# Two weight panels over one token chunk at the head of a decoder step

## The chip, the cores and the metric

The kernel runs on one core of a Trainium2 chip. The metric is the device time of one execution in microseconds (us). A core has a matrix engine (TensorE, PE in the profile, with its weight loads as PEld), a vector engine (DVE), a scalar engine (ACT), GpSimd (POOL) and SyncE (SP), whose queue issues the DMA transfers of this part of the kernel. Each engine works through its own queue in order and waits there for the work of others.

## The reference

One inference step of a decoder layer over 1024 prompt tokens and 8 x 8 sample tokens, with D_MODEL = 1024:

```python
u = rmsnorm(x);  [a | q | k | v | g_a | g_b] = u @ w_in
# branch A: causal pooling of a (4 groups of 128 channels, windows 2/4/8/16),
#           (mean - a) -> linear map per group -> scale -> @ w_pa
# branch B: dilated window attention on q, k, v -> @ w_pb
h = x + (sigmoid(g_a) * A + sigmoid(g_b) * B) @ w_o
y = h + relu(rmsnorm(h) @ w_up)^2 @ w_down
```

The part that matters here is `a`, the pooling input: 512 channels, that is two panels of 256 columns of w_in, for all 1088 tokens. The row norm of x is not applied before the product: x is scaled by the norm weight alone, and the factor for each token, taken from its sum of squares, comes in later.

## The kernel before

Features lie on the partitions: x arrives as eight rows of 128 features, each with all tokens, and the tokens are cut into three chunks of 384, 384 and 320 (`CHUNKS`). Every product is made from two-part numbers: ACT makes a rounded "high" copy and DVE the rest, "low", of each operand, and PE does three passes (high x high, high x low, low x high: `PASSES`). For x this is `split_x` (lines 297 and 298, one row of one chunk each), for weights `split` (lines 114 and 115, one raw tile of 512 columns, that is two feature rows of a panel).

A panel of w_in comes in four raw tiles (line 123), which rotate through three buffers, and its halves are kept in one of three `places`. For the first panel `panel` calls `first(j)` between the fetch and the split of each raw tile: it loads the two x rows that belong to it and splits them. Row 0 and the small table `cols` are loaded ahead (lines 278 and 279), row 1 by line 304, the others in pairs by line 281.

`pool_input(ja, wt, c)` multiplies one panel by one chunk: for each pair of feature rows 12 matmuls (line 319: three passes, two column halves m, two rows kk), 48 for the whole. They collect in two PSUM banks of the four `acc` banks, and `pool_evac` copies these to `ext` on ACT (lines 331 and 336).

The order on PE is the order of the code. It is: twelve warm-up matmuls on `ones` (line 345); panel 0 on chunks 0, 1, 2; panel 1 on chunks 0, 1, 2; then the first products of the q, k, v panels (lines 611, 614 and 194). Between the chunks of panel 1 stand the token sums `x_sums(c)` (line 354): after chunk 0 `x_sums(0)`, after chunk 1 `x_sums(1)` and a small transpose `wk`, and inside chunk 2, after 36 of its 48 matmuls, `x_sums(2)`.

`x_sums(c)` needs the squares of chunk c. ACT squares x in place (line 289, four instructions for a chunk, held back until the matmuls that stand before them in the code have ended), POOL adds the four up (line 291, three for a chunk). PE then sums over the partitions into three small PSUM tiles `rt`, which all three calls share; DVE reads them (line 358, `xms`), and POOL makes the power of it (line 359, `rtok`). `sample_rows` copies the sample tokens on DVE (line 269).

The queues of ACT, DVE, POOL and SP are not written by hand: a scheduler lays them out when the kernel is built, from a model of the timeline, and the order is then fixed.

Of the kernel before, what the change touches and what calls it, by code (L numbers as in the profile page):

```python
# [7 lines left out]
F32 = mybir.dt.float32  # L8
# [7 lines left out]
P = 128  # L16
# [4 lines left out]
KD = D // P  # L21
CH = 384
CHUNKS = ((0, 384), (384, 384), (768, 320))
# [13 lines left out]
def decoder_step(ctx, tc, i, o):  # L37
    nc = tc.nc
    v_, s_, g_, t_ = nc.vector, nc.scalar, nc.gpsimd, nc.tensor
    dma = nc.sync.dma_start  # L40
    dma_st = nc.sync.dma_start

    def pool(name, bufs=1, **kw):
        return ctx.enter_context(tc.tile_pool(name=name, bufs=bufs, **kw))
# [44 lines left out]
    def part4(c):  # L89

        return slice(CHUNKS[c][0] // 4, (CHUNKS[c][0] + CHUNKS[c][1]) // 4)
# [16 lines left out]
    wp = pool("w")  # L108
    places = wp.tile([P, 3, 2, 2048], F32R, name="places")
    place = [0]  # L110
    throttle = []

    def split(dst_hi, dst_lo, src):
        ins = s_.activation(dst_hi, src, AF.Copy)
        v_.tensor_tensor(dst_lo, src, dst_hi.bitcast(F32), op=ALU.subtract)  # L115
        return ins
# [43 lines left out]
    def panel(src, name, between=None, after=None):  # L160

        n = src.shape[1]
        wt = places[:, place[0] % 3]
        place[0] += 1
        for a in range(0, n, 512):
            raw = fetch(src, name, a)
            if between is not None:
                between(a // 512)
            ins = split(wt[:, 0, a:a + 512], wt[:, 1, a:a + 512], raw)
            if after is not None:  # L170
                behind_pe(ins, after[a // 512])
        throttle.append(ins)
        return wt

    def by_k(wt, kb=KD):
        return wt.rearrange("p s (k n) -> p s k n", k=kb)
# [59 lines left out]
    def acc_tile(name, tag="acc", bufs=4):  # L236
        return rr(acc_p, [P, 512], F32, name, tag, bufs)
# [55 lines left out]
    def split_x(c, k):  # L293
        c0, n = CHUNKS[c]
        hi, lo = (act4[s][k][:, :, part4(c)] for s in range(2))
        x = xs[c, k].rearrange("p (l r) -> p r l", r=4)
        s_.activation(hi, x, AF.Copy, scale=ln1[:, k:k + 1])  # L297
        v_.scalar_tensor_tensor(lo, x, ln1[:, k:k + 1], hi.bitcast(F32), op0=ALU.mult, op1=ALU.subtract)

    def first(j):  # L300
        if j:
            load_x(0, j)
        else:
            dma(xs[0, 1], i["xT"][:, 1, :CH])
        split_x(0, 2 * j)
        split_x(0, 2 * j + 1)

    L = 15 + SEQ
    LS = L + NB * 23
# [2 lines left out]
    def pool_input(ja, wt, c, middle=None):  # L312
        c0, n = CHUNKS[c]
        pts = [acc_tile(f"a{2 * ja + m}_{c}") for m in range(2)]
        for k in range(0, KD, 2):
            for p, (a, b) in enumerate(PASSES):
                for m in range(2):
                    for kk in (k, k + 1):
                        last_mm[0] = t_.matmul(  # L319
                            pts[m][:, :n], wt[:, a, kk, m * P:(m + 1) * P], act4[b][kk][:, :, part4(c)],  # L320
                            start=(p == 0 and kk == 0), stop=(p == 2 and kk == KD - 1))
            if middle and k == 4:
                middle()
        return pts

    def pool_evac(ja, c, pts):
        c0, n = CHUNKS[c]
        for m in range(2):
            ext = exts[2 * ja + m]
            npr = min(n, SEQ - c0)  # L330
            s_.copy(ext[:, 15 + c0:15 + c0 + npr].rearrange("p (l r) -> p l r", r=4),
                    from4(pts[m][:, :n])[:, :npr // 4])
            if npr < n:
                new = from4(pts[m][:, :n])[:, npr // 4:].rearrange("p (t q) r -> p q r t", q=2)
                for q in range(2):
                    s_.copy(ext[:, L:].rearrange("p (b t) -> p b t", b=NB)[:, 4 * q:4 * q + 4, 15:], new[:, q])

    def open_ext(g):
        exts[g] = rr(xp, [P, LS], F32, name=f"ext{g}", tag="ext", bufs=4)
        v_.memset(exts[g][:, :15], 0.0)  # L340


    wu = rr(ps, [P, 512], F32, name="wu", tag="wu", bufs=1)[:, :P]
    for _ in range(12):
        t_.matmul(wu, ones, ones, start=True, stop=True)
    load_x(0, 0)
    wt = by_k(panel(i["w_in"][0], "a0", first))
    def x_sums(c):
        n = CHUNKS[c][1]
        rt = [rr(ps, [P, 1], F32, name=f"rt{c}_{b}", tag="rt", bufs=3) for b in range(3)]  # L350
        for b in range(3):
            w = min(P, n - b * P)
            for k in range(2):
                t_.matmul(rt[b][:w], xs[c, 6 + k][:, b * P:b * P + w], ones[:, :1], start=(k == 0), stop=(k == 1))
        for b in range(3):
            w = min(P, n - b * P)
            col = slice(3 * c + b, 3 * c + b + 1)
            v_.tensor_scalar(xms[:w, col], rt[b][:w], 1.0 / D, EPS, op0=ALU.mult, op1=ALU.add)
            g_.tensor_tensor(rtok[0][:w, col], xms[:w, col], mhalf[:w, :1], op=ALU.pow)
            v_.tensor_scalar(xeps[0][:w, col], xms[:w, col], EPS, None, op0=ALU.mult)  # L360
# [36 lines left out]
    for c in range(3):  # L397
        if c < 2:
            for j in range(4):
                load_x(c + 1, j)  # L400
        if c == 0:
            open_ext(0)
            open_ext(1)
        pool_evac(0, c, pool_input(0, wt, c))
        if c < 2:
            for k in range(KD):
                split_x(c + 1, k)
        if c:
            square_x(c - 1)
    square_x(2)  # L410
    w1 = by_k(panel(i["w_in"][1], "a1"))
    dma(cst, i["consts"])
    v_.tensor_scalar(wqs, wqc, HD ** -0.5, None, op0=ALU.mult)
    dma(states, i["stateT"].rearrange("g p b t -> p g (b t)"))
    kn = win("kn")[:, :P]
    for g in range(3):
        dma(kn[2 * g:2 * g + 2], i["qk_norm"][g, 1].rearrange("(j d) -> j d", j=2))
    open_ext(2)
    open_ext(3)
    for c in range(3):  # L420
        pool_evac(1, c, pool_input(1, w1, c, (lambda: x_sums(2)) if c == 2 else None))
        if c == 0:
            x_sums(0)
            sample_rows()
        if c == 1:
            x_sums(1)

            wk = rr(ps, [P, 512], F32, name="wk", tag="wu", bufs=1)[:, :6]
            t_.transpose(wk, kn[:6], ident[:6, :6])
            v_.tensor_tensor(wqk, wqs, wk, op=ALU.mult)  # L430
# [676 lines left out]
    for g in (2, 1, 0):  # L1107
# [39 lines left out]
        for blks in ((8, 0), (1,), (2,), (3,), (4,), (5,)) + (((6, 7),) if g else ((6,), (7,))):  # L1147
# [10 lines left out]
            for js in (((0, 1), (2,)) if blks[0] in (1, 2, 3, 4, 5) else ((0,), (1,), (2,))):  # L1158
                for b in (blks[::-1] if g == 0 and js == (2,) else blks):
# [307 lines left out]
    for n, (f, a) in enumerate(order):  # L1467
# [5 lines left out]
        t = row_tile(1 + a, f)  # L1473
# [187 lines left out]
    for j in range(2):  # L1661
        for d in range(4):
            wt = by_k(panel(i["w_o"][d], f"o{j}{d}"))
# [251 lines left out]
    kept, hs, rows, chain = {}, {}, {}, []  # L1915
# [246 lines left out]
```

## Time and profile before

| what | us |
|---|---|
| time, median of 3 runs | 1431.8 (1431.59 to 1432.39) |
| the profiled execution, its own time | 1434.28 |
| its span, first to last instruction | 1432.1 |
| PE busy in the span | 1410.9 |
| DVE busy | 976.4 |
| ACT busy | 758.7 |
| POOL busy | 225.5 |

Times in the profile count from the start of the span. The profiled execution is 2.5 us above the median of the runs and its span is 2.2 us shorter than its own time. PE is busy for 99% of the span, but busy time of pipelined matmuls says nothing on whether they follow one another closely; for the head of the kernel the instructions themselves have to be read.

### The profile page before, as it was taken

The page shows a single profiled execution, that of the slowest core. Times are in us where ns is not written, and L with a number is a line of the kernel's source. Part 1 is how long each engine was busy: PE and PEld are TensorE (multiplying, and loading weights), DVE is VectorE, ACT ScalarE, POOL GpSimd, SP SyncE. Part 2 cuts the span into 40 slices and gives each one's busy share as a digit, 9 for nine tenths or more (in the row PEclk, how much of TensorE's full clock was granted, in tenths as well). Part 3 has the DMA queues.
Part 4 walks back from the last instruction along what each step waited for, and adds up shares of the span by engine and source line. Part 5 has one row for each costly group of instructions (what it writes and reads, how often), then busy time and mean ns, then how long its engine had stood idle before and what let it go on. Part 6 is the DMA issues. An engine that isn't in the chain of part 4 may idle for free.

```text
span 1432.1 us, 29419 instructions
## 1 busy us (share of the span) xinstructions
PE 1410.9 (99%) x11101; PEld 1358.0 (95%) x11101; DVE 976.4 (68%) x1795; ACT 758.7 (53%) x1962; POOL 225.5 (16%) x291
## 2 busy tenths in 40 slices
PE   9999999999989999999999999999999999999998
PEld 8988977887989999999999999999999999999998
DVE  7688675676768677786468876666665686664556
ACT  8557755687755233573336545554554544444442
POOL 0711255565400000000001000000000000000100
PEclk9999999999999999999999999999999999999999
DMA  6322888854576686974558667656658987777684
GB/s 211 115 80 108 222 210 213 199 134 113 127 226 213 207 260 192 331 265 151 168 174 256 231 221 230 210 203 230 224 189 283 319 272 257 234 241 222 208 279 155
DMA packets 184204, 300.01 MB, mean 209 GB/s; under 512 B 34423, under 2 KB 91069, under 8 KB 182014
## 3 DMA queue, kind: packets, MB, share of 16 engines
q1 hardware_dynamic: 180990, 254.49, 57.5%
q0 software_dynamic: 3072, 43.65, 9.3%
q8 instruction: 87, 1.43, 0.4%
q14 instruction: 55, 0.45, 0.1%
HBM read 229.66 MB, written 112.06 MB: 239 GB/s over the span
## 4 chain that ended last, share of the span: by engine, by line
PE 85%; DMA 6%; DVE 4%; ACT 2%; issue 2%; SPq 1%; POOL 1%; DVEq 0%; ACTq 0%; POOLq 0%
PE pz L1249 22%; PE pd L2021 21%; PE pg L1249 10%; PE ph L194 7%; PE pqk L194 6%; PE pv L194 4%; PE a L319 3%; PE pab L1567 2%; PE pq L194 1%; PE pk L194 1%; DMA gg<-g_d 1%; DMA gv<-ts_d 1%; DVE places L115 1%; DVE act L115 1%; DMA out_yT_dram<-row 1%
## 5 line engine op out<-in xcount | busy, mean ns | idle before, releaser
L2021 PE MATMUL pd<-places 128*128 128x272 f32 x2688 | 335.2, 287 | 1.4 <-DVE places L1257 1.0
L2021 PEld LDWEIGHTS pd<-places 128*128 128x128 f32 x2688 | 334.7, 188 | 1.8 <-DVE places L1257 1.2
L1256 ACT ACTIVATE places<-raw_d 128x544 fp32r<-128x544 f32 (+1 forms) x176 | 111.0, 646 | 156.4 <-DMA raw_d<-z_d 48.3
L1257 DVE TENSOR_TENSOR places<-raw_d,places 128x544 fp32r<-128x544 f32 (+1 forms) x176 | 122.5, 710 | 88.5 <-ACT places L1256 87.3
L2060 POOL DMA_DIRECT2D out_kv_sample_dram<-in_cache_kv_dram x96 | 47.0, 490 | 832.0 <-ACT places L1256 538.0
L1249 PE MATMUL pz<-act,places 128*128 128x272 f32 x912 | 119.2, 289 | 0.0
L1249 PEld LDWEIGHTS pz<-act,places 128*128 128x128 f32 x912 | 116.5, 188 | 0.0
L194 PE MATMUL ph<-act,places 128*128 128x272 f32 x768 | 97.0, 288 | 0.0
L194 PEld LDWEIGHTS ph<-act,places 128*128 128x128 f32 x768 | 96.5, 188 | 0.1
L1249 PE MATMUL pg<-act,places 128*128 128x272 f32 x576 | 79.8, 297 | 2.4 <-ACT g L1475 2.4
L1249 PE MATMUL pz<-act,apart 128*128 128x272 f32 x624 | 82.0, 289 | 0.0
L1249 PEld LDWEIGHTS pz<-act,apart 128*128 128x128 f32 x624 | 79.9, 188 | 0.1
L1249 PEld LDWEIGHTS pg<-act,places 128*128 128x128 f32 x576 | 76.4, 195 | 3.2 <-ACT g L1475 2.6
L634 POOL TENSOR_TENSOR mr<-ms,mhalf 128x4 f32<-128x4 f32 (+2 forms) x39 | 54.1, 1387 | 109.7 <-DVE ms L633 109.6
L194 PE MATMUL pqk<-places,act 128*128 128x512 f32 x240 | 61.0, 403 | 0.0
L1249 PE MATMUL pz<-places 128*128 128x272 f32 x432 | 56.4, 287 | 0.0
L1249 PEld LDWEIGHTS pz<-places 128*128 128x128 f32 x432 | 55.0, 188 | 0.0
L839 POOL TENSOR_TENSOR pck<-pck,qs 128x256 f32<-128x256 f32 x64 | 48.4, 788 | 36.7 <-DMA pck<-in_cache_kv_dram 22.0
L194 PEld LDWEIGHTS pqk<-places,act 128*128 128x128 f32 x240 | 44.6, 192 | 9.9 <-issue 0.2
L319 PE MATMUL a<-act,places 128*128 128x384 f32 (+1 forms) x288 | 50.5, 332 | 1.1 <-ACT act L297 1.1
L1567 PE MATMUL pab<-ab,places 128*128 128x272 f32 x384 | 50.5, 287 | 0.0
L319 PEld LDWEIGHTS a<-act,places 128*128 128x128 f32 x288 | 47.5, 188 | 3.0 <-ACT act L297 1.9
(438 smaller groups left out, 2864.2 us busy)
## 6 DMA issues: line engine op xcount, KB each, us to landing
out_kv_sample_dram<-in_cache_kv_dram POOLq DMA_DIRECT2D x72, 480.0 KB, 4.9
raw_d<-z_d SPq DMA_DIRECT2D x112, 272.0 KB
z_d<-t SPq DMA_DIRECT2D x84, 272.0 KB
raw_d<-in_w_down_dram SPq DMA_DIRECT2D x80, 256.0 KB
raw_u<-in_w_up_dram SPq DMA_DIRECT2D x64, 256.0 KB
raw_qkv<-in_w_in_dram SPq DMA_DIRECT2D x36, 256.0 KB
pck<-in_cache_kv_dram SPq DMA_DIRECT2D x32, 256.0 KB
pcv<-in_cache_kv_dram SPq DMA_DIRECT2D x32, 256.0 KB
```

The costliest lines, as they stand in the source:

```text
L115: v_.tensor_tensor(dst_lo, src, dst_hi.bitcast(F32), op=ALU.subtract)
L194: last_mm[0] = t_.matmul(out, lhs(a, k), rhs(b, k), start=(j == 0), stop=(j == len(terms) - 1))
L319: last_mm[0] = t_.matmul(pts[m][:, :n], wt[:, a, kk, m * P:(m + 1) * P], act4[b][kk][:, :, part4(c)], start=(p == 0 and kk == 0), stop=(p ...
L634: g_.tensor_tensor(r[:n, :H], ms[:n, :H], mhalf[:n, :H], op=ALU.pow)
L839: behind_pe(g_.tensor_tensor(t[:, n], t[:, n], qs[:, :256], op=ALU.mult))
L1249: last_mm[0] = t_.matmul(x[c][:, :Q], A[:, a, k * P:(k + 1) * P], Bv(b, k, c), start=(first and n == 0), stop=(n == len(terms) - 1), skip_ ...
L1256: ins = s_.activation(view(t[:, 0]), src, AF.Copy)
L1257: v_.tensor_tensor(view(t[:, 1]), src, view(t[:, 0]).bitcast(F32), op=ALU.subtract)
L1567: last_mm[0] = t_.matmul(q[x][:, c, :Q], w.rearrange("p s n -> p (s n)")[:, at:at + P], rhs, start=(n == 0), stop=(n == len(terms) - 1))
L2021: last_mm[0] = t_.matmul(chain[t][:, c, :Q], A[:, a, t * P:(t + 1) * P], Z[:, b, c * Q:(c + 1) * Q], start=(fresh and f == 0 and n == 0), ...
L2060: ins = g_.dma_start(d, a)
```

## The change

The two panels of `a` are loaded in turns, raw tile by raw tile, and both multiply chunk 0 together: for each pair of feature rows the 12 matmuls of panel 0, then the 12 of panel 1. Chunk 0 so takes four PSUM banks. Then panel 0 does chunks 1 and 2, and panel 1 chunks 1 and 2. The very first raw tile is loaded and split in two halves of one feature row each; x row 0 is split with the first half, and x row 1 is loaded behind both halves and split with the second. For that first pair of panel 0 the 12 matmuls go row by row: six for row 0, six for row 1. There are ten warm-up matmuls. `x_sums(0)` moves to the middle of panel 1 on chunk 1, `x_sums(1)` and `sample_rows` follow after that chunk, and `x_sums(2)` stays in the middle of chunk 2.

```diff
-    def first(j):
+    def first(j, rows):
         if j:
             load_x(0, j)
-        else:
+        elif 1 in rows:
             dma(xs[0, 1], i["xT"][:, 1, :CH])
-        split_x(0, 2 * j)
-        split_x(0, 2 * j + 1)
+        for m in rows:
+            split_x(0, 2 * j + m)
...
         for k in range(0, KD, 2):
+            pool_terms(pts, wt, c, k)
+            if middle and k == 4:
+                middle()
+        return pts
+
+    def pool_terms(pts, wt, c, k, by_row=False):
+        n = CHUNKS[c][1]
+        for ks in ((k,), (k + 1,)) if by_row else ((k, k + 1),):
             for p, (a, b) in enumerate(PASSES):
                 for m in range(2):
-                    for kk in (k, k + 1):
+                    for kk in ks:
...
-    for _ in range(12):
+    for _ in range(10):
         t_.matmul(wu, ones, ones, start=True, stop=True)
     load_x(0, 0)
-    wt = by_k(panel(i["w_in"][0], "a0", first))
+    two_wide = [places[:, n] for n in range(2)]
+    place[0] = 2
+    for n in range(4):
+        for j in range(2):
+            raw = rr(wp, [P, 512], F32, name=f"raw_a{j}_{n}", tag="raw", bufs=3)
+            parts = (slice(0, 256), slice(256, 512)) if n + j == 0 else (slice(0, 512),)
+            for cs in parts:
+                dma(raw[:, cs], i["w_in"][j][:, 512 * n + cs.start:512 * n + cs.stop])
+            for m, cs in enumerate(parts):
+                if j == 0:
+                    first(n, (m,) if parts[1:] else (0, 1))
+                split(*(two_wide[j][:, s, 512 * n + cs.start:512 * n + cs.stop] for s in range(2)), raw[:, cs])
+    wt, w1 = (by_k(t) for t in two_wide)
...
         if c == 0:
-            open_ext(0)
-            open_ext(1)
-        pool_evac(0, c, pool_input(0, wt, c))
+            for g in range(4):
+                open_ext(g)
+            pts = [acc_tile(f"a{m}_0") for m in range(4)]
+            for k in range(0, KD, 2):
+                for j, w in enumerate((wt, w1)):
+                    pool_terms(pts[2 * j:2 * j + 2], w, 0, k, k + j == 0)
+            for j in range(2):
+                pool_evac(j, 0, pts[2 * j:2 * j + 2])
+        else:
+            pool_evac(0, c, pool_input(0, wt, c))
...
-    w1 = by_k(panel(i["w_in"][1], "a1"))
...
-    for c in range(3):
-        pool_evac(1, c, pool_input(1, w1, c, (lambda: x_sums(2)) if c == 2 else None))
-        if c == 0:
-            x_sums(0)
+    for c in (1, 2):
+        pool_evac(1, c, pool_input(1, w1, c, lambda: x_sums(2 if c == 2 else 0)))
+        if c == 1:
             sample_rows()
-        if c == 1:
             x_sums(1)
```

More of the change, by code (lines that the diff above doesn't have):

```diff
@@ L321, in pool_input @@
                             start=(p == 0 and kk == 0), stop=(p == 2 and kk == KD - 1))
-            if middle and k == 4:
-                middle()
-        return pts
     def pool_evac(ja, c, pts):
@@ L417, in decoder_step @@
         dma(kn[2 * g:2 * g + 2], i["qk_norm"][g, 1].rearrange("(j d) -> j d", j=2))
-    open_ext(2)
-    open_ext(3)
-    for c in range(3):
-        pool_evac(1, c, pool_input(1, w1, c, (lambda: x_sums(2)) if c == 2 else None))
-        if c == 0:
-            x_sums(0)
+    for c in (1, 2):
+        pool_evac(1, c, pool_input(1, w1, c, lambda: x_sums(2 if c == 2 else 0)))
+        if c == 1:
             sample_rows()
-        if c == 1:
             x_sums(1)
```

## The prediction

> **What bounds the kernel now.** I read the page first: the chain that ended last is PE's for 85% of the span. Then I read that chain in order of time over the first 85 us, where the change lies (columns: start, us, what).
>
> ```profile
> PE 85%; DMA 6%; DVE 4%; ACT 2%; issue 2%; SPq 1%; POOL 1%; DVEq 0%; ACTq 0%; POOLq 0%
> ...
> 3.09 5.59 DMA xs<-in_xT_dram
> 8.70 1.86 ACT act L297 x2
> 10.60 30.83 PE a L319 x179
> 41.43 1.23 PE rt L354 x12
> 42.66 8.64 PE a L319 x48
> ...
> 59.27 1.96 PE a L319 x12
> ```
>
> Up to 10.6 us the chain is x rows 2 and 3: their transfer, then their two high copies. From there it does not leave PE until the pooling input ends at 61.2 us. So the head ends when PE's matmuls end, and time can be won only where PE waits among them. The weight loads, in order of time, show where; they break wherever a matmul had to wait (start, length, engine, line, instruction, count, idle before).
>
> ```profile
> 1.06 5.13 PEld L345 LDWEIGHTS wu<-ones 128*128 128x128 f32 x24 [1.06 <-DVE ones L73]
> 6.15 0.19 PEld L319 LDWEIGHTS a<-act,places 128*128 128x128 f32 x1
> 7.24 0.65 PEld L319 LDWEIGHTS a<-act,places 128*128 128x128 f32 x4 [0.90 <-ACT act L297]
> 8.19 1.18 PEld L319 LDWEIGHTS a<-act,places 128*128 128x128 f32 x7 [0.30 <-DVE act L298]
> 9.73 0.19 PEld L319 LDWEIGHTS a<-act,places 128*128 128x128 f32 x1 [0.37 <-ACT act L297]
> 10.60 0.65 PEld L319 LDWEIGHTS a<-act,places 128*128 128x128 f32 x4 [0.68 <-ACT act L297]
> 11.55 2.04 PEld L319 LDWEIGHTS a<-act,places 128*128 128x128 f32 x12 [0.30 <-DVE act L298]
> 13.86 1.17 PEld L319 LDWEIGHTS a<-act,places 128*128 128x128 f32 x7 [0.27 <-DVE act L298]
> 15.18 25.93 PEld L319 LDWEIGHTS a<-act,places 128*128 128x128 f32 x156 [0.15 <-ACT places L114]
> ...
> 52.62 5.28 PEld L319 LDWEIGHTS a<-act,places 128*128 128x128 f32 x36
> 57.86 1.33 PEld L354 LDWEIGHTS rt<-ones,xs 128*128 128x128 f32 x12
> ```
>
> From 15.18 us on PE is dense. The 36 loads in 5.28 us are of the 320-token chunk: 0.147 us each. Of the 156 loads in 25.93 us, 48 are of that chunk (7.06 us), so the other 108, of 384 tokens, take 0.175 each. Ahead of 15.18 lie 1+4+7+1+4+12+7 = 36 matmuls, 6.3 us of dense work. PE therefore behaves **as if it had begun at 15.18 - 6.3 = 8.9 us** and never waited. I call this the dense start. The first matmul starts at 6.15; the 2.7 us between are waits for splits. All of the gain of the head is a lower dense start.
>
> **The change part by part.** No matmul of the product goes away: chunk 0 takes 96 in a row instead of 48 and 48. What changes is when each is ready. ACT, DVE and SP at the start (all from the timeline of the head):
>
> ```profile
> 2.14 0.43 SPq L304 DMA_DIRECT2D xs<-in_xT_dram  x1
> 2.61 0.43 SPq L123 DMA_DIRECT2D raw_a<-in_w_in_dram  x1
> 3.46 0.98 ACT L297 ACTIVATE act<-xs,cols 128x384 fp32r<-128x384 f32 x1 [1.22 <-DMA cols<-in_cols_dram]
> 4.48 0.90 DVE L298 SCALAR_TENSOR_TENSOR act<-xs,cols,act 128x384 fp32r<-128x384 f32 x1 [0.91 <-ACT act L297]
> 5.47 0.63 ACT L114 ACTIVATE places<-raw_a 128x512 fp32r<-128x512 f32 x1 [1.03 <-DMA raw_a<-in_w_in_dram]
> 6.21 0.98 ACT L297 ACTIVATE act<-xs,cols 128x384 fp32r<-128x384 f32 x1
> 8.70 1.85 ACT L297 ACTIVATE act<-xs,cols 128x384 fp32r<-128x384 f32 x2 [0.35 <-DMA xs<-in_xT_dram]
> ```
>
> *Warm-up and first half.* Twenty loads of 0.214 us (5.13 / 24) end at 1.06 + 4.28 = 5.3 us instead of 6.2. Row 0 is split by 4.44 (high) and 5.38 (low). The first half of the weights lands between 3.4 us (the table `cols`, issued before it, was there by 3.46) and 5.47 (the whole tile was). Its high copy costs between half of 0.63 and 0.63; I take 0.37. So six matmuls can go from about 5.4 us. These two edits by themselves give nothing more, since the later rows decide; uncovered, the two warm-ups would be worth 0.9 us.
>
> *Row 1.* Its transfer is issued one slot, 0.47 us, later (behind the second half, at 2.61). Its high copy ran at 6.21, right behind another copy, so it had landed by then; now I take 6.4 (5.9 to 6.7), high done at 7.4, low at 8.3. The ninth matmul is the first that needs the low part, so the dense start is at least 8.3 - 8 x 0.175 = 6.9.
>
> *Rows 2 and 3.* Ahead of their transfer now stands one more weight tile. It costs between one SP slot (0.47 us) and that plus its 256 KB at the rate of the head:
>
> ```profile
> 5.00:10.00 5.00, 4.31 (x21) 3.35 (x19) 2.96 (x5) 3.55 (x5) 0.00 (x0) 1.00 1.01 343
> 10.00:15.00 5.00, 4.58 (x23) 3.82 (x23) 5.00 (x7) 5.00 (x7) 0.00 (x0) 1.00 1.07 377
> ```
>
> At 360 GB/s (last column) that is 0.7 us, so the high copies start between 9.2 and 9.9 instead of 8.70; I take 9.4. Row 3 is then high at 9.4 + 1.85 = 11.25 and low 0.9 later, 12.15. 24 matmuls stand ahead of this pair, so the thirtieth is the first that needs the low part of row 3: dense start 12.15 - 29 x 0.175 = **7.1** (6.9 to 7.6). For later pairs ACT needs 2 x 0.93 + 2 x 0.57 = 3.0 us (1.85 / 2 above, 1.13 / 2 below) and PE has 24 x 0.175 = 4.2 us of work, the 896 KB of a pair and its two weight tiles arrive in 2.5 us, so PE does not wait again in chunk 0. Before, ACT needed 2.4 us for each 2.1 us of PE. That is the mechanism of the gain: **8.9 - 7.1 = 1.8 us**.
>
> *Four banks.* Panel 0 of chunk 1 needs the banks of panel 0 of chunk 0, which end 12 matmuls, 2.1 us, before the chunk does. Their two copies take 0.82 (below). I cost it at nothing; behind other copies on ACT it would be up to 0.8.
>
> *Squares and token sums.* All splits of panel 1 and two more bank copies now stand on ACT ahead of the squares, and POOL's additions hang on these.
>
> ```profile
> 20.35 0.82 ACT L331 COPY ext<-a 128x384 f32<-128x384 f32 x2
> 21.08 7.98 ACT L297 ACTIVATE act<-xs,cols 128x384 fp32r<-128x384 f32 x10
> 30.74 3.04 ACT L289 ACTIVATE xs<-xs 128x768 f32<-128x768 f32 x4
> 33.69 1.13 ACT L114 ACTIVATE places<-raw_a 128x512 fp32r<-128x512 f32 x2
> ...
> 32.40 16.71 POOL L291 TENSOR_TENSOR xs<-xs,xs 128x768 f32<-128x768 f32 x8 [31.95 <-ACT xs L289]
> 49.83 2.55 POOL L359 TENSOR_TENSOR rtok<-xms,mhalf 128x1 f32<-128x1 f32 x3 [0.71 <-DVE xms L358]
> 52.34 2.32 POOL L291 TENSOR_TENSOR xs<-xs,xs 128x640 f32<-128x640 f32 x1
> ```
>
> The squares of chunk 0 started at 30.74. Ahead of them come 1.13 (two splits that were behind), 0.82 (copies) and about 0.1 for the split cut in two, 2.05 us; ACT's waits for x add between 0 and 1.2 us (later transfers, less the split that fills the gap), I take 0.3. They start at 33.1, above PE's gate at 7.1 + 144 x 0.175 = 32.3. POOL's last addition then ends at 52.34 + 2.32 + 2.35 = 57.0, if POOL keeps its order. PE wants it at 57.86 - 1.8 = 56.1. Slack before: 3.2 us; after: none, and a wait of **0.9 us** (0.6 to 1.8).
>
> Sum: -1.8 + 0.9 = **-0.9 us**. Behind the head PE stays the bound, so it passes on to the end. The profiled execution would take 1433.4 us instead of 1434.28; it lies 2.5 above the median of the runs, so I forecast 1430.9. Queues of the later stages may be laid out anew; the largest single wait of PE there is
>
> ```profile
> PE pv L194 <- ACT qk L639: 2.8, 1, 2.8
> ```
>
> so I allow, as an estimate, 1 us to either side.
>
> **The clock.** The warm-up loads take 0.214 us for 128 columns; a later product of the same kind, 2 records of 384 columns in 0.65 us, takes 0.108. PE thus runs at half rate at the start, though the clock column prints 1.00. Later the granted clock (third column from the right) falls to 0.51 for 3.5 us, behind 7 us in which PE was busy for 4.48 only:
>
> ```profile
> 66.65 0.65 PE bcx L244 x2
> ...
> 395.00:402.00 7.00, 4.48 (x47) 4.16 (x45) 2.35 (x8) 1.72 (x6) 0.00 (x0) 1.00 1.06 371
> 402.00:405.50 3.50, 3.50 (x18) 2.95 (x14) 2.90 (x16) 2.36 (x9) 0.00 (x0) 0.51 0.95 241
> ```
>
> [...]
>
> **The rivals.**
>
> *POOL steps aside.* If its powers of chunk 0 (2.55 us) are queued behind the additions, the last one ends by 54.5, before 56.1, and all 1.8 us stay: 1430.0. For it: they become ready later, since `x_sums(0)` moves from 41.4 to 7.1 + 180 x 0.175 + 7.1 = 45.7. Against: one addition stood behind them before.
>
> *A clean start.* If rows 1 to 3 come early enough that PE never waits after the warm-up, the dense start is 5.4 and, with POOL clear, 3.5 us are gained: 1428.3. Against: row 3 must be high 1.5 us sooner than I reckon, with more bytes ahead of it.
>
> *The token sums block PE (slower).* `x_sums(1)` writes the tiles that DVE must have read for chunk 0. Before, 48 matmuls lay between; now 12, 2.1 us.
>
> ```profile
> 34.34 4.63 DVE L115 TENSOR_TENSOR places<-raw_a,places 128x512 fp32r<-128x512 f32 x2 [2.49 <-ACT places L114]
> 49.60 0.15 DVE L358 TENSOR_SCALAR xms<-rt 128x1 f32<-128x1 f32 x1
> ```
>
> DVE read the first at 49.60, 6.9 us after the sums ended at 42.66, being behind splits that took 2.3 us each while POOL added. With the same lag PE waits 6.9 - 2.1 = 4.8 us: -1.8 + 4.8 = +3.0, **1434.8**. It decides from a lag of 3.9 us. Against: fewer splits lie between POOL's start and these sums, which now come 4 us later.
>
> *The clock opens late.* If the shorter warm-up costs one more stretch like that of 402 us, 3.5 us at 0.51, PE loses 1.7 us: +0.8, 1432.6. Against: the waits of 0.90 and 0.68 us did not slow the matmuls then.
>
> **How the numbers follow.** Forecast 0.45, POOL aside 0.20, clean start 0.12, token sums 0.13, clock 0.10. About 0.2%, 2.9 us, is what a measurement of this kernel can tell from no change. Faster by more: most of the clean start, and the edge of POOL aside with the 1 us: 0.20. Slower by more: the token sums and an edge: 0.14. Within: 0.66. The range runs from the clean start less half a microsecond, 1427.8, to just below the token sums' full price, 1434.6; some 0.17 is left out.
>
> **What would show it.** The break in the weight loads for row 3 at about 11.3 to 12.2 us and a long dense run after it give the dense start (7.1); the first squares of ACT at 33 and POOL's last addition at 57 show the give-back, together with an idle time of PE before the third group of `rt` loads. An idle time before the second group would be the token sums blocking. Loads of 0.3 us beyond 6.5 us would be the clock. I am wrong if rows 1 to 3 land elsewhere, or if the scheduler puts POOL's or SP's queue in another order.

## The result: 15 us slower

| | before | after |
|---|---|---|
| median of six runs, us | 1431.86 (1429.9 to 1433.12) | 1447.13 (1443.06 to 1449.19) |
| ratio, 95% interval | | 1.0104 (1.0087 to 1.012) |
| the profiled execution, its own time | 1434.28 | 1445.87 |
| its span | 1432.1 | 1443.7 |

I forecast 1430.9 us, in a range from 1427.8 to 1434.6. The change costs 15.3 us, and both its sign and its size lie outside. First the weight loads of the changed kernel, in order of time (columns as before; L327 is the product of the pooling input, L371 the token sums):

```profile
8.59 3.63 PEld L327 LDWEIGHTS a<-act,places 128*128 128x128 f32 x21 [0.65 <-DVE act L298]
12.52 1.17 PEld L327 LDWEIGHTS a<-act,places 128*128 128x128 f32 x7 [0.30 <-DVE act L298]
13.88 2.03 PEld L327 LDWEIGHTS a<-act,places 128*128 128x128 f32 x12 [0.19 <-ACT places L114]
19.65 6.72 PEld L327 LDWEIGHTS a<-act,places 128*128 128x128 f32 x24 [3.74 <-ACT places L114]
30.37 28.45 PEld L327 LDWEIGHTS a<-act,places 128*128 128x128 f32 x156 [4.00 <-ACT places L114]
...
62.62 1.41 PEld L371 LDWEIGHTS rt<-ones,xs 128*128 128x128 f32 x12 [0.32 <-POOL xs L291]
...
70.26 1.29 PEld L371 LDWEIGHTS rt<-ones,xs 128*128 128x128 f32 x12 [0.78 <-POOL xs L291]
```

Up to 13.88 us the head is what I reckoned with: 36 matmuls lie ahead of that row, so the dense start is 13.88 - 36 x 0.175 = 7.6 us, against 8.9 before. Then two waits of 3.74 and 4.00 us follow, both for the high copies of weights. And the loads behind them are slow: the 24 take 6.72 us instead of 24 x 0.175 = 4.2, and the 156 take 28.45 instead of the 25.93 of before. The windows of the changed kernel say why (span of the window, then PE, PEld, DVE, ACT, POOL busy; third from the right is the granted clock):

```profile
20.00:25.00 5.00, 5.00 (x17) 5.00 (x17) 5.00 (x8) 5.00 (x7) 0.00 (x0) 0.50 0.94 321
25.00:30.00 5.00, 1.69 (x9) 1.37 (x7) 5.00 (x8) 5.00 (x8) 0.00 (x0) 0.84 0.01 3
30.00:35.00 5.00, 4.63 (x14) 4.63 (x15) 3.10 (x7) 2.38 (x6) 0.00 (x0) 0.50 0.43 122
```

Behind each of the two waits PE runs at half clock (0.50). In the window from 25 to 30 us, in which PE mostly waits, ACT and DVE are busy without a break, and the transfers stand still (3 GB/s). So PE waits for ACT, and ACT isn't idle: it does something else first. ACT's queue, in order:

```profile
13.69 5.39 ACT L297 ACTIVATE act<-xs,cols 128x384 fp32r<-128x384 f32 x6
18.99 1.13 ACT L114 ACTIVATE places<-raw_a 128x512 fp32r<-128x512 f32 x2
20.03 9.77 ACT L297 ACTIVATE act<-xs,cols 128x384 fp32r<-128x384 f32 x12
29.71 1.13 ACT L114 ACTIVATE places<-raw_a 128x512 fp32r<-128x512 f32 x2
...
46.14 3.06 ACT L289 ACTIVATE xs<-xs 128x768 f32<-128x768 f32 x4
```

Counted in the order of the code, the six x splits at 13.69 are rows 6 and 7 of chunk 0 and four rows of chunk 1; the twelve at 20.03 are the rest of chunk 1 and all of chunk 2. PE needs these chunks only after 96 matmuls. They stand ahead of the weights of feature rows 4, 5 and of rows 6, 7, which PE waits for. SP's queue is mixed in the same way:

```profile
10.45 4.45 SPq L281 DMA_DIRECT2D xs<-in_xT_dram  x6
...
20.77 0.36 SPq L359 DMA_DIRECT2D raw_a<-in_w_in_dram  x1
```

The six transfers at 10.45 are, in the same order, x of chunks 1 and 2. The last raw tile of panel 1, number 7 of 0 to 7, is issued at 20.77 only: with three buffers it takes over that of tile 4, which ACT splits at 18.99, behind its six x splits. So one order feeds the other: a late split frees a buffer late, the transfer starts late, and its own split stands behind twelve more.

How far the head ends late can be read where the streams are alike again, at the first 24 loads of the v panel. Before:

```profile
74.83 2.96 PEld L194 LDWEIGHTS pv<-places,act 128*128 128x128 f32 x24
```

After:

```profile
88.73 2.96 PEld L194 LDWEIGHTS pv<-places,act 128*128 128x128 f32 x24
```

That is +13.9 us, which I call **the head's lag**. It is made of -1.3 (the dense start), +7.7 (the two waits, 3.74 and 4.00), +2.5 and +2.5 (half clock behind them), +1.1 (the waits of 0.32 and 0.78 at the token sums) and +1.4 (half clock once more, at 73.1 us for 3.4 us). The chain of waits of the changed kernel agrees: up to 30.37 us it no longer runs over PE but over ACT's x splits.

```profile
13.83 5.25 ACT act L297 x6
20.12 9.68 ACT act L297 x12
30.37 28.78 PE a L327 x156
```

### The profile page after: what moved, and what is told of

Same layout as the page of the kernel before. It is cut to its first block, busy times and chain, and to the rows that moved or that the text cites. A ratio compares the mean times of both kernels' runs of the same rounds, so it can differ in the third digit from the quotient of the medians.

```text
span 1443.7 us, 29423 instructions
## 1 busy us (share of the span) xinstructions
PE 1415.5 (98%) x11097; PEld 1361.5 (94%) x11097; DVE 971.6 (67%) x1796; ACT 758.0 (53%) x1963; POOL 222.7 (15%) x291
## 4 chain that ended last, share of the span: by engine, by line
PE 83%; DMA 6%; DVE 4%; ACT 3%; issue 1%; POOL 1%; SPq 1%; DVEq 0%; POOLq 0%; ACTq 0%
PE pz L1268 22%; PE pd L2040 22%; PE pg L1268 11%; PE ph L194 7%; PE pqk L194 5%; PE pv L194 3%; PE a L327 2%; PE pab L1586 2%; ACT act L297 1%; PE pq L194 1%; DMA pcv<-in_cache_kv_dram 1%; PE pk L194 1%; DMA raw_qkv<-in_w_in_dram 1%; DMA out_yT_dram<-row 1%; DMA gx<-in_xT_dram 1%
## 5 line engine op out<-in xcount | busy, mean ns | idle before, releaser
L327 PE MATMUL a<-act,places 128*128 128x384 f32 (+1 forms) x288 | 55.6, 355 | 8.5 <-ACT places L114 7.1
L327 PEld LDWEIGHTS a<-act,places 128*128 128x128 f32 x288 | 52.5, 205 | 10.5 <-ACT places L114 7.9
```

The source lines that it names most:

```text
L327: last_mm[0] = t_.matmul(pts[m][:, :n], wt[:, a, kk, m * P:(m + 1) * P], act4[b][kk][:, :, part4(c)], start=(p == 0 and kk == 0), stop=(p ...
```

## The experiments

The theory that I formed from this: **two panels go through three raw buffers while the scheduler is free to put later chunks of x ahead of them**. Rivals: the small edits (halves, rows, ten warm-ups) do it; the half clock does it; the x splits' place on ACT alone does it, whatever the buffers. The twelve kernels in one table, each beside runs of the kernel before on the same chip:

| kernel | median, us | before there | ratio (95%) | head's lag |
|---|---|---|---|---|
| e1_held | 1444.73 | 1430.86 | 1.0101 (1.0078 to 1.0124) | +14.3 |
| e2_five | 1437.89 | 1430.86 | 1.0049 (1.003 to 1.0068) | +4.9 |
| e3_fill | 1442.35 | 1430.86 | 1.0088 (1.0069 to 1.0106) | +11.9 |
| e4_apart | 1432.47 | 1430.86 | 1.002 (1.0008 to 1.0033) | -0.2 |
| e5_banks | 1437.88 | 1431.93 | 1.0051 (1.003 to 1.0073) | +6.5 |
| e6_squares | 1434.34 | 1431.93 | 1.0024 (1.0012 to 1.0036) | +0.9 |
| e7_adds | 1435.06 | 1431.93 | 1.0024 (1.0012 to 1.0035) | +2.1 |
| e8_two_only | 1444.73 | 1431.93 | 1.0094 (1.0076 to 1.0112) | +13.1 |
| e9_early | 1439.56 | 1431.59 | 1.0048 (1.003 to 1.0066) | +7.2 |
| e10_early_rows | 1438.98 | 1431.59 | 1.0053 (1.0033 to 1.0072) | +7.4 |
| e11_read | 1433.35 | 1431.54 | 1.0026 (1.001 to 1.0042) | +1.2 |
| e12_read_all | 1438.62 | 1430.34 | 1.0051 (1.0032 to 1.0071) | +5.0 |

The lag is the start of those 24 loads in the kernel's profile less 74.83. It agrees with the difference of the medians to within 2.2 us in all but the last (8.3 against 5.0). Behind the head the profiled executions differ as well: from 270 to 300 us the mean granted clock was 0.89 in the one before, 1.00 in the changed kernel and 0.94 in e9_early, from 390 to 450 us 0.94, 0.91 and 1.00. The ratio is not the quotient of the two medians, and where runs scatter the two differ: for e11_read the medians give 1.0013, the ratio is 1.0026.

### Which part does it: e8_two_only and e4_apart

e8_two_only keeps the two panels together and drops the three small edits; e4_apart keeps these and drops the two panels.

```diff
 # e8_two_only, against after
-    for _ in range(10):
+    for _ in range(12):
-            parts = (slice(0, 256), slice(256, 512)) if n + j == 0 else (slice(0, 512),)
+            parts = (slice(0, 512),)
-                    pool_terms(pts[2 * j:2 * j + 2], w, 0, k, k + j == 0)
+                    pool_terms(pts[2 * j:2 * j + 2], w, 0, k)
```

> The changed kernel without the small edits: whole first weight tile, rows 0 and 1 together, twelve warm-up matmuls; the two panels still take chunk 0 together from three raw buffers. Theory (the two panels from three buffers are the cause): both long waits stay and the time is that of the changed kernel, 1443 to 1449 us. Rival (the small edits are what shifts the queues): 1436 us or less.

> The kernel before with only the small edits: first weights in two halves, first rows feature by feature, ten warm-up matmuls; the panels take the chunks one after the other as before. Theory A: these edits cost and gain nearly nothing, since row 3 and ACT decide the dense start; within 1 us of before, 1431 to 1433 us. Rival (the small edits hurt, through smaller transfers or an early half-rate clock): 1435 us or more.

The two panels alone give 12.8 of the 15.3 us (1444.73 - 1431.93), with waits of 1.88, 2.00 and, the longest, 6.32 us for weights:

```profile
30.21 6.22 PEld L327 LDWEIGHTS a<-act,places 128*128 128x128 f32 x24 [6.32 <-ACT places L114]
```

The small edits alone gain nothing. In e4_apart the third token sums start at 57.70, 0.16 us earlier than before's 57.86. Its time is even 0.2% above before, with a head that isn't later; where that lies I didn't find.

### Order or buffers: e1_held and e2_five

e1_held leaves three buffers and queues the x splits of chunks 1 and 2 on ACT and DVE behind the last weight split of the two panels.

```diff
...
+    hold = ins.ins, last_low[0].ins
...
+            with tc.issue_after(hold[0]), tc.issue_after(hold[1]):
-            for k in range(KD):
-                split_x(c + 1, k)
+                for k in range(KD):
+                    split_x(c + 1, k)
```

> The changed kernel, with the x splits of chunks 1 and 2 queued on ACT and DVE behind the last weight split of chunk 0; buffers, transfers and PE order are untouched. Theory A (the fixed order of ACT's queue): the two long waits of PE (3.7 us before matmul 49, 4.0 us before matmul 73) come from weight splits queued behind x splits of later chunks. The first wait goes; of the second about 2.7 us stay, because the tile in question lands only at 21.8 us in the changed kernel; the time falls from 1447 to 1434 to 1438 us. Theory B (late transfers alone): the splits wait for their tiles and not for ACT, so reordering ACT changes little, 1443 to 1448 us. Theory C (clock alone): the waits are small and the half-rate clock is the cost; 1443 to 1448 us.

The time hardly moved; theory A, which put it at 1434 to 1438 us, failed. The two waits for weights shrank to 0.26 and 2.68 us, but two new ones came (1.51 and 5.71 us), for the copies of the PSUM banks (L337):

```profile
23.70 5.75 PEld L328 LDWEIGHTS a<-act,places 128*128 128x128 f32 x24 [2.68 <-ACT places L115]
30.96 0.30 PEld L328 LDWEIGHTS a<-act,places 128*128 128x128 f32 x2 [1.51 <-ACT ext L337]
36.96 23.74 PEld L328 LDWEIGHTS a<-act,places 128*128 128x128 f32 x130 [5.71 <-ACT ext L337]
```

On ACT one reads the reason:

```profile
23.02 0.63 ACT L115 ACTIVATE places<-raw_a 128x512 fp32r<-128x512 f32 x1 [5.65 <-DMA raw_a<-in_w_in_dram]
...
30.79 5.76 ACT L298 ACTIVATE act<-xs,cols 128x384 fp32r<-128x384 f32 x7
36.45 0.47 ACT L337 COPY ext<-a 128x384 f32<-128x384 f32 x1
```

With the x splits out of the way ACT idles 5.65 us for a raw tile, which SP issues at 15.99 only, still behind six transfers of x. And the x splits, now late, stand ahead of the bank copies. Mending ACT's order alone takes 4.8 us off the waits for weights and adds 7.2 us of others.

e2_five gives the eight raw tiles five buffers and leaves all orders to the scheduler.

```diff
-            raw = rr(wp, [P, 512], F32, name=f"raw_a{j}_{n}", tag="raw", bufs=3)
+            raw = (rr(xq, [P, 512], F32, name=f"raw_a{j}_{n}", tag="rawx", bufs=2) if 2 * n + j in (3, 4)
+                   else rr(wp, [P, 512], F32, name=f"raw_a{j}_{n}", tag="raw", bufs=3))
```

> The changed kernel with five instead of three raw buffers for the two panels; no order is forced, the scheduler lays out the queues itself. Theory A' (three buffers for two panels are the root: the tile that needs the fourth buffer is issued late, the scheduler's model then fills ACT with x splits of later chunks): both long waits and both stretches of half clock go, the dense start is 7 us as predicted and the time 1429 to 1433 us. If the squares on ACT and POOL give time back as predicted, PE waits 0.6 to 1.8 us at the third token sums. Rival (the two panels together cost by themselves, through four banks, late squares or more ACT work): 1436 us or more.

Both waits for weights are gone. From its break at 12.64 us the dense start is 12.64 - 29 x 0.175 = 7.6, and the scheduler itself has put the weight splits ahead of chunk 1. SP issues all raw tiles ahead of the x of chunks 1 and 2, the last by 10.3 us instead of 20.77:

```profile
8.49 1.85 SPq L360 DMA_DIRECT2D raw_a<-in_w_in_dram  x2
10.39 5.21 SPq L281 DMA_DIRECT2D xs<-in_xT_dram  x8
```

Two thirds of the lag are gone too, but only about half of the time: it is still 7.0 us above the kernel before, in the range of the rival and not of theory A'. These rows hold what is left:

```profile
26.78 21.93 PEld L327 LDWEIGHTS a<-act,places 128*128 128x128 f32 x132 [2.15 <-ACT ext L336]
...
54.38 1.41 PEld L372 LDWEIGHTS rt<-ones,xs 128*128 128x128 f32 x12 [2.20 <-POOL xs L291]
...
55.96 6.82 PEld L327 LDWEIGHTS a<-act,places 128*128 128x128 f32 x36
```

2.15 us for the bank copies, 2.20 for POOL's additions, and 36 loads in 6.82 us instead of 5.28, which I take for half clock again. So three buffers were the root of the two waits for weights; what I had costed at nothing ("Four banks") comes next.

### What the clock takes: e3_fill

e3_fill is the changed kernel with 14 matmuls on `ones` ahead of the k = 4 and the k = 6 pairs of chunk 0, so that PE idles less while it waits. They are work that nobody reads.

```diff
             for k in range(0, KD, 2):
+                for _ in range(14 if k > 2 else 0):
+                    t_.matmul(wu, ones, ones, start=True, stop=True)
```

> The changed kernel with 14 idle matmuls on ones (3.0 us at full rate) ahead of the matmuls that wait longest, twice; ACT, DVE and DMA are as in the changed kernel. If the clock falls because PE idles there, PE keeps the full rate: the 24 matmuls after the first wait take 4.2 instead of 6.7 us, the 156 after the second 26 instead of 28.5, and the time falls by 4 to 6 us, to 1441 to 1443 us. If the slow stretches have another cause (data, contention), nothing is gained: 1446 to 1449 us.

```profile
19.94 4.11 PEld L327 LDWEIGHTS a<-act,places 128*128 128x128 f32 x24 [0.55 <-ACT places L114]
...
30.65 4.46 PEld L327 LDWEIGHTS a<-act,places 128*128 128x128 f32 x26 [3.35 <-ACT places L114]
35.28 21.56 PEld L327 LDWEIGHTS a<-act,places 128*128 128x128 f32 x130 [0.17 <-ACT ext L336]
```

The 24 loads take 4.11 us instead of 6.72, and the 156 take 26.0 instead of 28.45: the half clock in these two places was the idle time's doing. But the first 2.6 us don't reach the end, since the second wait ends when ACT ends it, at 30.65 here and at 30.37 in the changed kernel. The lag falls by 2.0 us. By the ratios the time falls by 0.16%, 2.3 us, and by the medians, each less its own before, by 3.8; both are below the 4 to 6 that I had expected. So of 15 us some 2 to 4 hang on the clock in these two places. The sum of the lag above counts 5.0 for them; but without the first stretch the second wait would have been as much longer.

### After the buffers: e5_banks, e6_squares, e7_adds

Each of these mends what the one before it still showed, to see whether the predicted gain is below. `issue_after` queues what stands in it behind an instruction, on the same engine; `emptied`, `squared`, `added` and (further below) `read` list the bank copies, squares, additions and DVE's reads of the token sums in the order of the code.

```diff
 # e5_banks: e2_five, and the x splits of rows 5 to 7 of chunk 1 and of chunk 2 behind the first bank copies on ACT
...
+            early = 5 if c == 0 else 0
+            for k in range(early):
+                split_x(c + 1, k)
+            with tc.issue_after(emptied[1].ins):
+                for k in range(early, KD):
+                    split_x(c + 1, k)
 # e6_squares: e5_banks, and the splits of the q, k, v weights behind the squares of chunk 0 on ACT
+            with tc.issue_after(squared[3].ins):
                 for j in range(3):
                     panel(i["w_in"][4 + 3 * j], f"qkv2_{j}")
 # e7_adds: e6_squares, and POOL does the additions chunk by chunk, and every power behind them
...
+            with tc.issue_after(added[8].ins):
+                g_.tensor_tensor(rtok[0][:w, col], xms[:w, col], mhalf[:w, :1], op=ALU.pow)
```

> Five raw buffers as in e2, and on ACT the x splits of rows 5 to 7 of chunk 1 and all of chunk 2 are queued behind the two copies that empty the banks of panel 0. Theory (what is queued ahead on ACT sets PE's waits, one after the other): the wait of 2.15 us at the start of chunk 1 goes. But the squares then still stand behind weight splits that wait for transfers, POOL adds as late as in e2, and PE waits that much longer at the second token sums (2.2 us in e2, now 3 to 4.5), so the time stays within 1.5 us of e2, 1436 to 1439 us. Rival (each wait counts by itself): about 2 us less than e2, 1434 to 1436 us.

In e5_banks the product is dense for 199 loads, but the time doesn't move, as expected: the squares are as late as in e2_five (38.58 against 38.20), and PE waits for POOL's additions.

```profile
54.50 2.30 PEld L374 LDWEIGHTS rt<-ones,xs 128*128 128x128 f32 x12 [4.29 <-POOL xs L291]
```

> As e5, and the weight splits of the q, k, v panels are queued behind the squares of chunk 0 on ACT. Theory: the squares start at 33 to 35 us instead of 38.2, POOL's additions 4 us sooner, and the waits at the token sums shrink below 1.5 us together, so the time falls to 1431 to 1434 us. This is the state that the prediction reckoned with (dense start 7 to 7.6, squares at 33, a wait of about a microsecond at the token sums). Rival (something else than the order of the queues makes the two-panel start slow): 1436 us or more.

e6_squares comes nearest to the state that I had reckoned with: dense start 12.75 - 29 x 0.175 = 7.7, no wait for weights or banks, and a wait at the third token sums.

```profile
12.75 33.53 PEld L330 LDWEIGHTS a<-act,places 128*128 128x128 f32 x199 [0.32 <-DVE act L301]
...
58.81 1.29 PEld L377 LDWEIGHTS rt<-ones,xs 128*128 128x128 f32 x12 [1.87 <-POOL xs L294]
```

On POOL, its powers (L382) and its last addition in this kernel:

```profile
49.98 2.32 POOL L382 TENSOR_TENSOR rtok<-xms,mhalf 128x1 f32<-128x1 f32 x2
...
53.89 0.58 POOL L382 TENSOR_TENSOR rtok<-xms,mhalf 128x1 f32<-128x1 f32 x1
54.79 1.74 POOL L382 TENSOR_TENSOR rtok<-xms,mhalf 128x1 f32<-128x1 f32 x2 [0.32 <-DVE xms L381]
56.49 2.26 POOL L294 TENSOR_TENSOR xs<-xs,xs 128x640 f32<-128x640 f32 x1
```

It ends at 58.75, and PE's loads start at 58.81. I had 57.0 and a wait of 0.9; the wait is 1.87, and it takes back more than the 1.2 us of the dense start. The squares are hardly the reason, they start at 33.59 (forecast 33.1). POOL's order is: its first addition starts 2.9 us later than in the kernel before (35.27 against 32.40), but its last ends 4.1 later, and five powers stand ahead of that one, where the kernel before had three. The time, 1434.34, is just above the 1431 to 1434 that I expected here.

> As e6, and on POOL the additions stand in the order of the chunks with all powers behind them. Theory: no wait is left at the token sums, the head keeps the whole lower dense start, 1.3 us or more below before: 1429 to 1431.5 us. Rival: the powers now come late and hold back what follows the head (row factors), 1433 us or more.

In e7_adds no token sum waits, but PE waits 2.90 us at `mt`, and the time is in the rival's range:

```profile
62.80 1.35 DVE L115 TENSOR_TENSOR places<-raw_qkv,places 128x512 fp32r<-128x512 f32 x2 [3.90 <-ACT places L114]
64.07 0.27 DVE L384 TENSOR_SCALAR xms<-rt 128x1 f32<-128x1 f32 x3
...
64.72 0.30 PEld L417 LDWEIGHTS mt<-to,mv 128*128 128x128 f32 x2 [2.90 <-DVE mv L411]
```

The rival's reason, late powers, is not what the trace shows: `mt` needs `mv`, and `mv` is made from the token sums themselves (`xms`), not from their powers. DVE reads the third sums at 64.07 only, behind two weight splits that wait for ACT, which waits 5.72 us for a transfer of the q, k, v weights. It is the place that e11_read meets again below.

### The token sums' tiles: e9_early, e10_early_rows, e11_read, e12_read_all

```diff
 # e9_early: e6_squares, and the squares of a chunk wait for its own matmuls only
-        if c:
-            square_x(c - 1)
-    square_x(2)
+        square_x(c)
 # e10_early_rows: e9_early, and x rows 2 and 3 are loaded ahead of panel 1's first tile
+            load_x(0, 1)
 # e11_read: e9_early, and the k and v weights' splits behind DVE's read of the token sums of chunk 0
-            with tc.issue_after(squared[3].ins):
-                for j in range(3):
+            for j in range(3):
+                with tc.issue_after(read[2].ins if j else squared[3].ins):
 # e12_read_all: e11_read, and the k splits behind the read of chunk 1, the v splits behind that of chunk 2
+                with tc.issue_after((squared[3], read[5], read[8])[j].ins):
```

> Edit: the kernel of e6_squares, and the squares of each chunk are held back by one step of PE less: those of chunk 0 until its own matmuls have ended, not until panel 0 of chunk 1 has. Theory A (what is left of the loss is that POOL's additions start too late): squares of chunk 0 start at 25 to 34 us instead of 35, POOL's last addition ends before PE asks for the third token sums, no wait at the rt loads, dense start still 7.6 to 7.8, so the head is 1.2 us shorter than before's and the time 1430 to 1433, within 0.2% of before. Theory B (as in e7_adds: with the squares early POOL takes all powers behind the additions, and what reads the power waits): a wait of PE of some 2.7 us behind the head, 1433.5 to 1436.5. Theory C (the rest of the loss is not in the head at all): the head is shorter by 1.2 us and the time still 0.2% above before.

None of the three theories holds; theory B rested on late powers in e7_adds, which its trace doesn't bear out. The squares are early and POOL is done, but the second token sums wait 5.87 us:

```profile
55.56 2.64 PEld L377 LDWEIGHTS rt<-ones,xs 128*128 128x128 f32 x12 [5.87 <-POOL xs L294]
```

The view puts it down to POOL; POOL's additions of chunk 1 had ended at 45.6, though. DVE's queue shows the one that came last:

```profile
51.46 3.92 DVE L115 TENSOR_TENSOR places<-raw_qkv,places 128x512 fp32r<-128x512 f32 x2 [3.23 <-ACT places L114]
55.30 0.15 DVE L381 TENSOR_SCALAR xms<-rt 128x1 f32<-128x1 f32 x1
```

DVE reads the sums of chunk 0 at 55.30, 7.6 us after they were made (46.21 + 1.48 = 47.7), since two weight splits stand ahead of the read and wait for ACT, which does the squares of chunk 2 first. 7.6 less the 2.1 us of the 12 matmuls between gives 5.5. This is the rival "the token sums block PE" of the prediction, by its own sum.

> Edit: the kernel of e9_early, and x rows 2 and 3 are loaded right behind row 1, ahead of the first weight tile of panel 1. Theory A (the prediction's term: the one weight tile ahead of rows 2 and 3 costs the dense start 0.5 to 1.2 us): the splits of row 3 end 0.5 to 0.9 us sooner, dense start 6.8 to 7.1 instead of 7.7, time 0.4 to 0.8 us below e9_early. Theory B (the first weight tile of panel 1 is then what comes late): PE waits at the thirteenth matmul instead, dense start unchanged within 0.2 us, time the same as e9_early.

Theory B, and by the second break worse than it says. The rows of x come earlier (12 matmuls ahead of the break at 9.51: 9.51 - 12 x 0.175 = 7.4), but then PE waits for panel 1's weights, and again later, 72 matmuls in: 20.95 - 72 x 0.175 = 8.4.

```profile
9.51 10.36 PEld L331 LDWEIGHTS a<-act,places 128*128 128x128 f32 x60 [0.92 <-ACT places L114]
20.95 26.09 PEld L331 LDWEIGHTS a<-act,places 128*128 128x128 f32 x156 [1.09 <-ACT places L114]
```

> Edit: the kernel of e9_early, and the splits of the k and v panels' weights are queued on ACT and DVE behind DVE's third read of the token sums of chunk 0 (those of the q panel behind the squares of chunk 0, as before). Theory A (the wait of 5.9 us that e9_early brought at the second token sums is the three rt tiles, read late because DVE's queue had five to eight weight splits ahead of the reads): DVE reads them within 1 us of the sums' end, the wait at the second token sums is below 0.5 us, the half clock behind it goes too, no wait at the third, dense start 7.6 to 7.8; the head is then 1.0 to 1.4 us shorter than before's and the time 1430 to 1434 (ratio 0.999 to 1.002), 6 to 8 below e9_early. Theory B (the later splits then come too late for the k and v products): a new wait of PE at pk or pv of 1 to 4 us, 1433 to 1437. Theory C (the wait is POOL's additions of chunk 1 and not the tiles): wait unchanged within 1 us, time that of e9_early.

Theory A for the wait: it is gone, and the time falls by 6.2 us by the medians, 3.2 by the ratios (the lag by 6.0). That the tiles `rt` and DVE's order made it is thereby shown. Theory A's time, a ratio of 0.999 to 1.002, was missed by little (1.0026). Its head was missed by more: it was to be 1.0 to 1.4 us shorter than before's and is 1.2 longer. PE waits 0.53 us at the third token sums, whose tiles DVE reads at 57.32 only. Behind them the third read holds PE up:

```profile
62.59 0.69 DVE L115 TENSOR_TENSOR places<-raw_qkv,places 128x512 fp32r<-128x512 f32 x1 [1.94 <-ACT places L114]
63.20 0.28 DVE L383 TENSOR_SCALAR xms<-rt 128x1 f32<-128x1 f32 x3
```

It too stands behind a split that waits, and PE waits 1.28 us for what follows from it (`mt`).

> Edit: the kernel of e11_read, with the k panel's splits queued behind the read of the token sums of chunk 1 and the v panel's behind the read of chunk 2 (in e11_read both stood behind the first read). Theory A (the wait of 1.28 us at mt in e11_read is the third read, queued behind a weight split that waits for its tile): no wait at mt and none at the third token sums, the q products start 0.3 to 0.8 us earlier than before's (62.7 to 63.2 instead of 63.49) and the v products not later than before's (74.83); the time is 1430 to 1433, at most 0.1% above before; faster than before by more than 0.2% is not expected, since the whole term of the dense start is 1.2 us. Theory B (the k and v weights become late): a wait of 1 us or more at pk or pv, 1433 to 1436. Theory C (some 1 to 1.5 us of loss lie behind the head, as in e4_apart, which was 1.6 above before with its head 0.2 shorter): the head as in theory A and the time still 1 to 2 us above before.

Theory B, in another place than it named and dearer (it had 1433 to 1436). The wait at the third token sums is gone, and their loads start at 57.52, 0.3 us ahead of before. The wait at `mt` only shrank, from 1.28 to 0.85 us: a weight split that waits still stands ahead of the third read. And the weights that were held back kept the three raw buffers full, their transfers came late, and on ACT the copies that free the PSUM banks for the q products stand behind one of their splits:

```profile
66.05 0.63 ACT L114 ACTIVATE places<-raw_qkv 128x512 fp32r<-128x512 f32 x1 [2.33 <-DMA raw_qkv<-in_w_in_dram]
```

```profile
67.16 4.26 PEld L195 LDWEIGHTS pq<-places,act 128*128 128x128 f32 x24 [2.90 <-ACT ext L346]
```

PE waits 2.90 us and then does 24 loads in 4.26 us instead of 2.96. Some 3 us more are lost behind the head; I didn't follow them. No version beats the kernel before.

## Why the prediction was wrong, point by point

- **What bounds the kernel** was right for the kernel before, and the lag of the head gives the time to about 2 us. In the changed kernel the chain runs over ACT's splits up to 30.37 us.
- **Warm-up and first half**: right. Six matmuls went at 5.30 (forecast 5.4).
- **Row 1, rows 2 and 3**: right in mechanism, a little short in size. Row 1's high copy started at 6.62 (6.4), that of rows 2 and 3 at 9.66 (9.4). From the break at 12.52 the dense start is 12.52 - 29 x 0.175 = 7.4, inside 6.9 to 7.6; in the kernels of the same head it lies between 7.2 and 8.3. So the gain was 1.3 (with the 7.6 of the row at 13.88), not 1.8.
- **"For later pairs ... so PE does not wait again in chunk 0"**: this step failed. It compared rates: 3.0 us of ACT and 2.5 us of transfers against 4.2 us of PE for a pair. The rates were right, and e2_five shows that there is time enough. But I let ACT and SP work in the order of need, and it was laid out otherwise: with three buffers for eight tiles, eighteen x splits of which sixteen weren't yet needed stood ahead of the last four weight splits. It cost 7.7 us of waits where I had none, and twice 2.5 us at half clock behind them. My closing sentence named the queues of POOL and SP; the one that mattered first was ACT's. Why the scheduler's model saw no loss in that order I can't say from the traces.
- **"Four banks", costed at nothing**: in the changed kernel nearly so, because ACT had nothing left to do by then. As soon as the weights came in time, it cost 2.15 us (e2_five), not "up to 0.8": I had thought of other copies, and it was ten x splits.
- **Squares and token sums**: right in mechanism, 0.9 forecast. In the changed kernel 1.1 us are lost there, but with all of it shifted (squares at 46.14, not 33.1). In the state that I had reckoned with, e6_squares, it is 1.87, more than the gain: the squares were in time there, but my condition "if POOL keeps its order" didn't hold (five powers ahead of the last addition instead of three).
- **The rival "token sums block PE"** at 1434.8 had the right mechanism (e9_early, 5.9 us) and needed the squares early to come about. In the changed kernel the second sums wait only 0.32.
- **The rival "the clock opens late"** was about the wrong place. At the start of the changed kernel the full rate was there in time: the six loads at 5.30 took 1.00 us, 0.167 each. In e9_early, also with ten warm-ups, the first six took 1.72 us, 0.287 each, but there PE waited for row 1 behind them anyway. The clock's price, 2.5 us each time, came behind the waits of 3.7 and 4.0 us that I hadn't foreseen.
- **A clean start, POOL aside**: neither came. Rows 1 to 3 still set the dense start, and POOL's last addition ended at 70.21, 0.05 us ahead of the loads that wanted it. In e11_read POOL's additions did end early, at 55.43, and DVE's late reads of the sums took the gain instead.

## What to carry to other kernels

When an edit doubles what goes through a few rotating buffers, rates don't tell whether it will arrive; write out, for each engine's queue, what stands ahead of the item that PE waits for, and from which earlier item each buffer comes free. A queue that is laid out at build time can put work that is needed late ahead of work that is needed now, and mending one such place mostly moved the wait to the next one here. A gain of 1.3 us that hangs on four queues staying in order is worth less than one of these waits.

## What the runs showed of the hardware

PE's long waits in the head mostly cost more than their length here. Behind the waits of 3.74 and 4.00 us in the changed kernel the granted clock was 0.50 for 6.8 us each, and the 24 and the 156 loads that followed took 2.5 us longer, each time. Behind the five others from 4.29 to 6.32 us (e5_banks, e10_early_rows, e1_held, e9_early, e8_two_only) the loads took 2.1 to 3.0 us more than the same loads at the full rate took in other kernels, behind waits of 2.20 (e2_five), 2.68 (e1_held) and 2.90 us (e12_read_all) 1.3 to 1.6 us more. Behind waits of 1.87 (e6_squares), 1.88 and 2.00 (e8_two_only) and 2.15 us (e2_five: 132 loads in 21.93 us, 0.166 each) they took no longer. Length alone doesn't decide it: behind 2.90 us in e7_adds 24 loads took 2.96 us and behind 3.35 us in e3_fill, right behind the added matmuls, 26 took 4.46, both full rate. And behind the same 0.78 us at the third token sums the next 12 loads of the product took 1.91 us in the changed kernel, in which the clock fell at 73.12 us, 2.71 in e3_fill and 1.77, as without a wait, in e8_two_only.

In the changed kernel the granted clock falls at 18.50, 28.74 and 73.12 us and rises at 25.33, 35.57 and 76.53: in order, 2, 1, 2, 11 and 1 steps of 3.413 us apart. In the kernel before it falls at 285.98, 402.04 and 439.58 us and rises at 292.81, 405.45 and 443.00: 2, 32, 1, 10 and 1 of the same steps. The head of the changed kernel, cut along its grid (columns as in the windows above):

```profile
15.09:18.50 3.41, 1.14 (x7) 0.82 (x5) 3.41 (x5) 3.41 (x5) 0.00 (x0) 1.00 1.07 368
18.50:21.92 3.42, 2.27 (x7) 2.27 (x8) 3.42 (x5) 3.42 (x6) 0.00 (x0) 0.50 1.07 378
21.92:25.33 3.41, 3.41 (x13) 3.41 (x12) 3.41 (x6) 3.41 (x6) 0.00 (x0) 0.50 0.79 255
25.33:28.74 3.41, 1.36 (x8) 1.04 (x6) 3.41 (x6) 3.41 (x5) 0.00 (x0) 1.00 0.01 2
```

In these rows the clock is low behind the windows in which PE was busy for 1.14 and 1.36 us (behind the second at 28.74), and it rises behind the one that PE filled. Along the grids of both profiles, from the head to 1425 us, it fell behind windows with 0.40 to 1.47 us of PE's work (12 to 43%); the emptiest at a clock of 1.00 behind which it didn't fall held 1.63 us (48%, at 298.40 us of the changed kernel) and 1.82 (53%, at 419.10 us of the one before). One fall is apart from these: the window from 69.70 to 73.12 us of the changed kernel, with the third token sums in it, held 2.90 us.
